# Upper levels of a triangular inverse on 64x64 blocks instead of 128x128 in a hybrid decoder on one core

## The chip, the core and the metric

The kernel runs on one core of a Trainium2 chip, written in the Tile framework: the engines' instruction streams are laid out at build time by a scheduler, which follows the program's data dependences, a few orders pinned by hand, and its own estimate of what is ready first. At run time each engine works through its list in that order and waits where an operand or a buffer is not there. The engines are TensorE (PE, with its weight loads shown as PEld), VectorE (DVE), ScalarE (ACT) and GpSimd (POOL); SyncE (SP) issues the DMAs. The metric is device time in microseconds (us); the median over several runs counts.

## What is computed

The reference is a decoder trunk of two layers on x of 256 positions x 1024 channels. Each layer adds half a SwiGLU feed-forward, then a mix of four head groups, then another half feed-forward:

```
x = x + 0.5 * rms_norm(swiglu(h, w_gate, w_up, w_down), post_g)      # twice a layer, around:
p = h @ w_in
y_a = gate_b * causal_depthwise_conv(gate_c * xa, sc_conv_w)         # group A
y_b = spatial_gating(u, v, ...)                                       # group B
y_c = rwkv7_time_mix(pc, ...)                                         # group C: 4 heads of 64
zd  = causal_depthwise_conv(z1 * sigmoid(z2), cm_conv_w) + cm_conv_b  # group D: 31 taps
y_d = silu(layer_norm(zd, ...))
m   = concatenate([y_a, y_b, y_c, y_d]) @ w_out
```

Group C holds the recurrence in which the change lies:

```
sa = einsum("bhij,bhj->bhi", state, a_t)
state = state * w_t + sa[..., None] * b_t + v_t[..., None] * k_t
y = einsum("bhij,bhj->bhi", state, r_t)
```

## The kernel before

The 256 positions are two blocks (b = 0, 1) of 128. Every large product is made of three f32r matmuls with weights and activations split in a high and a low part (mm3, L148 to L150); ACT makes the high part of a weight (whi, L140) and DVE the low part (wlo, L141), from DMA buffers named raw. These casts go on all the time, for the stage that comes next too.

In the mix the recurrence of a block is solved in parallel form. c_pair builds, per head, 128x128 matrices: pp (L607) on row tiles of 64, masked into PB and PK. The inverse of a unit triangular 128x128 matrix is needed for each of 4 heads x 2 blocks. c_base solves its 16x16 diagonal blocks on DVE and writes them, transposed, into XM (L652). c_level(4), (5) and (6) then double the block size, 16 to 32, 64 and 128. A level is, for each block: zp = PB times XM (c_z, L670, four matmuls of 128x128, one a head), a copy zz on ACT (L673), wps = XT times zz (c_w, L685), and a write of the new off-diagonal blocks into XM, at level 4 by DVE under a mask (L692), at level 5 by two small ACT copies (L695). tx transposes the new XM on PE (xtp, L663) and ACT copies it to XT (L664). At level 6 only the transposed result is wanted, wps of L682, and ACT writes it straight to XT (L689).

Behind the levels comes a serial chain: c_u (x, L715, and u, L724), c_state (sp, S), the same of the second block, c_y (yp, L755 to L758), the group norm of yp (statistics st L767 and mv on DVE, rgn on POOL, yn on DVE, L773), its transposes ynT in c_out (L782), oc, and the product yh, yl that the output projection wo reads (emit_y, L437, L438). Group D shares the engines: its 31-tap convolution is a list of DVE steps (zc, L829), then zcT transposes (L835), a layer norm (dlnmv on DVE, dln on POOL, tk L838) and znT transposes (L842). Group B's gating needs sg matmuls (L898) and tk on DVE (L904).

wo has 96 matmuls of 512 columns a layer: per block, eight slices of 128 channels, in the order A, B, D, C (the list KORD at the foot of the file), two halves, three matmuls each. They are ready as soon as their group's yh and yl are, and the scheduler puts them where the chain leaves PE free. Program order around the change is: c_base, c_level(4), b_in(0), a_out(0), c_level(5), a_out(1), c_level(6), c_u, c_state, c_u, b_in(1), c_y twice, d_conv, c_out(1), d_out(0), c_out(0), d_out(1), wout.

Of the kernel before, what the change touches and what calls it, by code (L numbers as in the profile page):

```python
# [48 lines left out]
def trunk_kernel(ctx: ExitStack, tc: tile.TileContext, a, out):  # L49
# [48 lines left out]
    masks = const.tile([P, 3, P], U8, name="masks")  # L98
# [6 lines left out]
    def late_constants():  # L105
        mraw = work.tile([P, 3, P], mybir.dt.int32, name="mraw", tag="c2", bufs=C2)
        later(mraw, a["masks"])
        nc.vector.tensor_copy(masks, mraw)
# [300 lines left out]
    def mix(l, nxt):  # L409
# [18 lines left out]
        XM = zero_tile([P, NB, 4, P], "XM")  # L428
        XT = wp.tile([P, NB, 4, P], F32, name="XT", tag="w2", bufs=10)
# [191 lines left out]
        def c_base():  # L621
# [36 lines left out]

        def tx(b):
            S = R[b]  # L660
            tp = acc_bank("xtp")
            for h in range(4):
                nc.tensor.transpose(tp[:, h * P:(h + 1) * P], S["Xm"][:, h, :], ident)  # L663
            nc.scalar.copy(S["XT"], tp.rearrange("p (h t) -> p h t", h=4))  # L664

        def c_z(b):
            S = R[b]
            zp = acc_bank("zp")
            for h in range(4):
                nc.tensor.matmul(zp[:, h * P:(h + 1) * P], lhsT=PB[b][:, h, 1, :], rhs=S["Xm"][:, h, :],  # L670
                                 start=True, stop=True)
            z = work.tile([P, 4, P], F32, name="zz", tag="c2", bufs=C2)
            nc.scalar.copy(z, zp.rearrange("p (h t) -> p h t", h=4))  # L673
            S["z"] = z

        def c_w(b, i):
            S = R[b]
            w = acc_bank("wps")
            last = i == 6
            for h in range(4):  # L680
                if last:
                    nc.tensor.matmul(w[:, h * P:(h + 1) * P], lhsT=S["z"][:, h, :], rhs=S["XT"][:, h, :],  # L682
                                     start=True, stop=True)
                else:
                    nc.tensor.matmul(w[:, h * P:(h + 1) * P], lhsT=S["XT"][:, h, :], rhs=S["z"][:, h, :],  # L685
                                     start=True, stop=True)
            wv = w.rearrange("p (h t) -> p h t", h=4)
            if last:
                nc.scalar.copy(S["XT"][0:64, :, 64:P], wv[0:64, :, 64:P])  # L689
                return  # L690
            if i == 4:
# [431 lines left out]
```

## Time and profile before

| | |
|---|---|
| median of three runs | 1040.91 us (1040.3 to 1043.53) |
| profiled execution | 1042.24 us, span 1040.5 us, granted clock 0.998 |
| PE busy | 1016.9 us, 98% of the span |
| DVE, ACT, POOL busy | 670.5, 536.8, 68.8 us |
| levels of layer 1 | 280.03 us (first transpose) to 298.52 us (first x) |
| yn of the second block, layer 1 | starts at 315.87 us |
| last wo, first pgu of the next feed-forward | 332.07 and 332.30 us |

The span is the profiled stretch on the core, the execution's own time 1.74 us more. Layer 2 shows the same stretch 512 us later. The granted clock is that of TensorE as a share of full speed.

### The profile page before, as it was taken

The numbers are of one execution on the slowest core, as the hardware profiler recorded it, in microseconds if no ns is written. First come the engines' busy times: TensorE is split into PE (matmuls) and PEld (weight loads), VectorE is DVE, ScalarE is ACT, GpSimd is POOL, SyncE is SP. The second block draws the span as 40 slices with busy tenths as digits, with TensorE's granted clock in tenths as the row PEclk, the third lists the DMA queues.
The fourth block names the chain that finished last, engine by engine and source line by source line (L and its number), as shares of the span: only waits on it lengthen the run. The fifth ranks groups of instructions, "written<-read, shape, count | busy, mean of one in ns | idle before, by whom it ended". The sixth has DMA issues, their size and how long they took to land.

```text
span 1040.5 us, 13557 instructions
## 1 busy us (share of the span) xinstructions
PE 1016.9 (98%) x4898; PEld 831.4 (80%) x4898; DVE 670.5 (64%) x1084; ACT 536.8 (52%) x864; POOL 68.8 (7%) x133
## 2 busy tenths in 40 slices
PE   8999999999999999999999999999999999999997
PEld 6878888888797788888887888887878877888885
DVE  6664645689988746464675464547999885645442
ACT  7554444567466545444555454436655664535331
POOL 1000000210012100000010000003000130000000
PEclk9999999999999999999999999999999999999999
DMA  7984646344045756564647564635522366556521
GB/s 277 295 274 161 214 150 223 91 168 152 20 154 174 223 191 194 169 206 159 202 145 220 181 203 161 212 133 160 171 89 82 115 196 235 178 186 186 179 81 40
DMA packets 51474, 178.28 MB, mean 171 GB/s; under 512 B 6096, under 2 KB 6608, under 8 KB 51408
## 3 DMA queue, kind: packets, MB, share of 16 engines
q1 hardware_dynamic: 51120, 176.91, 52.1%
q8 instruction: 38, 0.62, 0.2%
q10 hardware_dynamic: 288, 0.52, 0.1%
q14 instruction: 28, 0.23, 0.1%
HBM read 176.36 MB, written 1.05 MB: 170 GB/s over the span
## 4 chain that ended last, share of the span: by engine, by line
PE 82%; DVE 7%; DMA 4%; ACT 2%; issue 2%; POOL 1%; SPq 1%; DVEq 0%; POOLq 0%; ACTq 0%
PE pgu L148 13%; PE pgu L149 13%; PE pgu L150 13%; PE dn L148 8%; PE dn L149 7%; PE dn L150 7%; DMA raw<-in_ffn 4%; PE pin L149 3%; PE pin L148 3%; PE pin L150 3%; PE hTp L344 2%; DVE wlo L141 1%; PE zp L670 1%; PE wo L148 1%; PE xT L178 1%
## 5 line engine op out<-in xcount | busy, mean ns | idle before, releaser
L141 DVE TENSOR_TENSOR wlo<-raw,whi 128x1024 fp32r<-128x1024 f32 (+1 forms) x320 | 389.0, 1219 | 135.5 <-ACT whi L140 121.2
L140 ACT CAST whi<-raw 128x1024 fp32r<-128x1024 f32 (+1 forms) x320 | 334.3, 1047 | 169.3 <-DMA raw<-in_ffn 76.7
L148 PE MATMUL pgu<-whi,xh 128*128 128x512 f32 x704 | 279.7, 398 | 1.8 <-ACT xh L237 1.5
L149 PE MATMUL pgu<-wlo,xh 128*128 128x512 f32 x704 | 276.5, 393 | 1.0 <-DVE wlo L141 0.8
L150 PE MATMUL pgu<-whi,xl 128*128 128x512 f32 x704 | 275.6, 392 | 0.0
L148 PEld LDWEIGHTS pgu<-whi,xh 128*128 128x128 f32 x704 | 132.6, 188 | 30.0 <-ACT xh L237 1.8
L150 PEld LDWEIGHTS pgu<-whi,xl 128*128 128x128 f32 x704 | 132.7, 188 | 28.7
L149 PEld LDWEIGHTS pgu<-wlo,xh 128*128 128x128 f32 x704 | 132.7, 188 | 28.3 <-DVE wlo L141 1.1
L148 PE MATMUL dn<-whi,hh 128*128 128x512 f32 x352 | 142.8, 407 | 2.7 <-ACT hh L347 2.7
L149 PE MATMUL dn<-wlo,hh 128*128 128x512 f32 x352 | 139.8, 397 | 0.0
L150 PE MATMUL dn<-whi,hl 128*128 128x512 f32 x352 | 138.2, 394 | 0.0
L335 ACT ACTIVATE silu<-pgu,rpre 128x256 f32<-128x256 f32 x88 | 41.6, 472 | 137.7 <-PE pgu L150 136.5
L337 DVE SCALAR_TENSOR_TENSOR h<-pgu,rpre,silu 128x256 f32<-128x256 f32 x88 | 42.4, 481 | 101.8 <-ACT silu L335 101.7
L348 DVE TENSOR_TENSOR hl<-hTp,hh 128x256 fp32r<-128x256 f32 x88 | 36.9, 419 | 89.4 <-ACT hh L347 89.4
L347 ACT CAST hh<-hTp 128x256 fp32r<-128x256 f32 x88 | 32.5, 369 | 97.4 <-PE hTp L344 97.4
L148 PEld LDWEIGHTS dn<-whi,hh 128*128 128x128 f32 x352 | 66.2, 188 | 18.2 <-ACT hh L347 4.0
L150 PEld LDWEIGHTS dn<-whi,hl 128*128 128x128 f32 x352 | 65.9, 188 | 17.2 <-DVE hl L348 1.5
L149 PEld LDWEIGHTS dn<-wlo,hh 128*128 128x128 f32 x352 | 66.2, 188 | 13.8 <-DVE wlo L141 0.4
L149 PE MATMUL pin<-wlo,xh 128*128 128x512 f32 (+2 forms) x192 | 70.8, 371 | 0.0
L148 PE MATMUL pin<-whi,xh 128*128 128x512 f32 (+2 forms) x192 | 70.5, 371 | 0.0
L150 PE MATMUL pin<-whi,xl 128*128 128x512 f32 (+2 forms) x192 | 70.5, 371 | 0.0
L829 DVE SCALAR_TENSOR_TENSOR zc<-zT,par,zc 128x256 f32<-128x256 f32 x120 | 49.9, 478 | 3.2 <-ACT zc L826 3.1
(216 smaller groups left out, 914.6 us busy)
## 6 DMA issues: line engine op xcount, KB each, us to landing
raw<-in_ffn SPq DMA_DIRECT2D x260, 512.0 KB, 4.6
raw<-in_wout SPq DMA_DIRECT2D x16, 512.0 KB, 4.3
raw<-in_win_z SPq DMA_DIRECT2D x8, 512.0 KB, 4.4
raw<-in_win_rk SPq DMA_DIRECT2D x8, 512.0 KB, 4.4
raw<-in_win_ca SPq DMA_DIRECT2D x8, 512.0 KB, 3.7
raw<-in_win_uv SPq DMA_DIRECT2D x8, 512.0 KB, 4.5
gp<-in_post_g SPq DMA_DIRECT2D x6, 512.0 KB, 4.7
raw<-in_win_vl SPq DMA_DIRECT2D x8, 384.0 KB, 3.1
```

The costliest lines, as they stand in the source:

```text
L140: i0 = nc.scalar.copy(hi[:, 0:n], raw[:, 0:n])
L141: i1 = nc.vector.tensor_tensor(out=lo[:, 0:n], in0=raw[:, 0:n], in1=hi.bitcast(F32)[:, 0:n], op=ALU.subtract)
L148: nc.tensor.matmul(dst, lhsT=sh, rhs=hi[:, c0:c0 + n], start=start, stop=False)
L149: nc.tensor.matmul(dst, lhsT=sh, rhs=lo[:, c0:c0 + n], start=False, stop=False)
L150: nc.tensor.matmul(dst, lhsT=sl, rhs=hi[:, c0:c0 + n], start=False, stop=stop)
L178: t = nc.tensor.transpose(tp[:, k * P:(k + 1) * P], x[b][:, kk * P:(kk + 1) * P], ident)
L335: nc.scalar.activation(out=s, in_=pg[:, 0:256], func=AF.Silu, scale=r)
L337: nc.vector.scalar_tensor_tensor(out=h, in0=pg[:, 256:512], scalar=r, in1=s, op0=ALU.mult, op1=ALU.mult)
L344: nc.tensor.transpose(tp[:, j * P:(j + 1) * P], h[:, j * P:(j + 1) * P], ident)
L347: nc.scalar.copy(hh, tp[:, 0:256])
L348: nc.vector.tensor_tensor(out=hl, in0=tp[:, 0:256], in1=hh.bitcast(F32), op=ALU.subtract)
L829: nc.vector.scalar_tensor_tensor(out=zc[:, j, :], in0=zT[:, j, k:k + 256], scalar=w, in1=zc[:, j, :], op0=ALU.mult, op1=ALU.add)
```

## The change

XM becomes a compact tile of 64 columns per head: the two 64x64 diagonal blocks of a head stand above one another, rows 0 to 63 and 64 to 127. XT stays a full tile and is now zeroed, since only its blocks are written. In levels 4 and 5 the matmuls work on 64x64 pieces: each of the array's four 64x64 quarters has its own piece, by the rows that its operands stand on and by the rows of the PSUM bank that it writes, so a head's two pieces and the heads go round all four, and write two banks instead of one (zp0, zp1; wps0, wps1). tx takes the compact XM of two heads as one 128x128 transpose, two a block instead of four, into a small tile xt2. tx_last, ahead of level 6, makes the transposes by 64x64 matmuls with the identity, so that they land in XT's diagonal blocks. Level 6 has one 64x64 product per head for z and one for w, all on the same quarter of the array. Level 4's mask, called near, covers 64 columns, and level 4 writes with two smaller predicated copies per block, level 5 with four ACT copies per block where there were two.

```diff
-        XM = zero_tile([P, NB, 4, P], "XM")
-        XT = wp.tile([P, NB, 4, P], F32, name="XT", tag="w2", bufs=10)
+        XM = work.tile([P, NB, 4, 64], F32, name="XM", tag="XM", bufs=1)
+        nc.gpsimd.memset(XM, 0.0)
+        XT = zero_tile([P, NB, 4, P], "XT")
...
         def tx(b):
             S = R[b]
             tp = acc_bank("xtp")
+            for g in range(2):
+                nc.tensor.transpose(tp[:, g * P:(g + 1) * P],
+                                    S["Xm"][:, 2 * g:2 * g + 2, :].rearrange("p h c -> p (h c)"), ident)
+            t = c256("xt2")
+            nc.scalar.copy(t, tp[:, 0:256])
+            S["X2"] = t.rearrange("p (g e c) -> p g e c", g=2, e=2)
+
+        def tx_last(b):
+            S = R[b]
+            tp = acc_bank("xtp")
             for h in range(4):
-                nc.tensor.transpose(tp[:, h * P:(h + 1) * P], S["Xm"][:, h, :], ident)
-            nc.scalar.copy(S["XT"], tp.rearrange("p (h t) -> p h t", h=4))
-
-        def c_z(b):
+                for e in range(2):
+                    nc.tensor.matmul(tp[half(e), 64 * h:64 * h + 64], lhsT=S["Xm"][half(e), h, :],
+                                     rhs=ident[half(e), half(e)], start=True, stop=True)
+            for e in range(2):
+                nc.scalar.copy(S["XT"][half(e), :, half(e)], tp[half(e), 0:256].rearrange("p (h c) -> p h c", h=4))
+
+        def c_z(b, i):
             S = R[b]
-            zp = acc_bank("zp")
+            if i == 6:
+                zp = acc_bank("zp")
+                for h in range(4):
+                    nc.tensor.matmul(zp[64:P, 64 * h:64 * h + 64], lhsT=PB[b][0:64, h, 1, 64:P],
+                                     rhs=S["Xm"][0:64, h, :], start=True, stop=True)
...
+            zp = [acc_bank("zp0"), acc_bank("zp1")]
             for h in range(4):
-                nc.tensor.matmul(zp[:, h * P:(h + 1) * P], lhsT=PB[b][:, h, 1, :], rhs=S["Xm"][:, h, :],
-                                 start=True, stop=True)
-            z = work.tile([P, 4, P], F32, name="zz", tag="c2", bufs=C2)
-            nc.scalar.copy(z, zp.rearrange("p (h t) -> p h t", h=4))
+                for e in range(2):
+                    c0 = 64 * (h // 2)
+                    nc.tensor.matmul(zp[e][half(h % 2), c0:c0 + 64], lhsT=PB[b][half(e), h, 1, half(e)],
+                                     rhs=S["Xm"][half(e), h, :], start=True, stop=True)
+            z = work.tile([P, 2, 2, 64], F32, name="zz", tag="c1", bufs=C1)
+            for e in range(2):
+                nc.scalar.copy(z[:, e], zp[e][:, 0:P].rearrange("p (g c) -> p g c", g=2))
             S["z"] = z
...
+            w = [acc_bank("wps0"), acc_bank("wps1")]
             for h in range(4):
...
+                for e in range(2):
+                    hh = half(h % 2)
+                    c0 = 64 * (h // 2)
+                    nc.tensor.matmul(w[h % 2][half(e), c0:c0 + 64], lhsT=S["X2"][hh, h // 2, e, :],
+                                     rhs=S["z"][hh, e, h // 2, :], start=True, stop=True)
+            for m in range(2):
+                wv = w[m][:, 0:P].rearrange("p (g t) -> p g t", g=2)
+                xv = S["Xm"].rearrange("p (g m) t -> p m g t", m=2)[:, m]
+                if i == 4:
+                    nc.vector.copy_predicated(out=xv, mask=near.unsqueeze(1).broadcast_to([P, 2, 64]), data=wv)
                 else:
-                    nc.tensor.matmul(w[:, h * P:(h + 1) * P], lhsT=S["XT"][:, h, :], rhs=S["z"][:, h, :],
-                                     start=True, stop=True)
...
+                    for q in (32, 96):
+                        nc.scalar.copy(xv[q:q + 32, :, 0:32], wv[q:q + 32, :, 0:32])
+            (tx if i == 4 else tx_last)(b)
```

The new shapes and durations give the scheduler another order. Three places of it matter below. On DVE, at level 4 (XM is the inverse being built, ao and yl belong to group A), the list was:

```order
L876 SCALAR_TENSOR_TENSOR ao<-caT,par,ao 128x128
L141 TENSOR_TENSOR wlo<-raw,whi 128x1024
L692 COPY_PREDICATED XM<-masks,wps 128x512
L879 TENSOR_TENSOR ao<-ao,gbT 128x256
L141 TENSOR_TENSOR wlo<-raw,whi 128x1024 x2
L692 COPY_PREDICATED XM<-masks,wps 128x512
```

and is now:

```order
L729 COPY_PREDICATED XM<-near,wps_2511 128x2x64
L729 COPY_PREDICATED XM<-near,wps_2512 128x2x64
L913 SCALAR_TENSOR_TENSOR ao<-caT,par,ao 128x128
L143 TENSOR_TENSOR wlo<-raw,whi 128x1024
L729 COPY_PREDICATED XM<-near,wps_2528 128x2x64
L729 COPY_PREDICATED XM<-near,wps_2529 128x2x64
L916 TENSOR_TENSOR ao<-ao,gbT 128x256
L143 TENSOR_TENSOR wlo<-raw,whi 128x1024 x2
```

The copies of the second block moved ahead of a product of group A and of two weight casts.

On DVE, from the convolution zc to the statistics st of yp (tk of L904 and L941 is group B's gating), the list was:

```order
L829 SCALAR_TENSOR_TENSOR zc<-zT,par,zc 128x256 x19
L141 TENSOR_TENSOR wlo<-raw,whi 128x1024
L904 SCALAR_TENSOR_TENSOR tk<-sg,par,uvt 128x64 x4
L141 TENSOR_TENSOR wlo<-raw,whi 128x1024
L800 BN_STATS st_2934<-zcT 128x6
L801 BN_AGGR dlnmv<-st_2934 128x2
L438 TENSOR_TENSOR yl_1750<-ybT,yh_1748 128x256
L838 TENSOR_SCALAR tk<-zcT,dlnmv,dln 128x256
L141 TENSOR_TENSOR wlo<-raw,whi 128x1024
L800 BN_STATS st_2988<-zcT 128x6
```

and is now, up to the second block's yn and a little beyond:

```order
L866 SCALAR_TENSOR_TENSOR zc<-zT,par,zc 128x256 x8
L941 SCALAR_TENSOR_TENSOR tk<-sg,par,uvt 128x64 x4
L866 SCALAR_TENSOR_TENSOR zc<-zT,par,zc 128x256 x3
L441 TENSOR_TENSOR yl_1753<-ybT,yh_1751 128x256
L866 SCALAR_TENSOR_TENSOR zc<-zT,par,zc 128x256 x8
L143 TENSOR_TENSOR wlo<-raw,whi 128x1024 x3
L804 BN_STATS st<-yp 128x6 x4
L806 BN_AGGR mv<-st 128x2 x4
L143 TENSOR_TENSOR wlo<-raw,whi 128x1024
L810 TENSOR_SCALAR yn<-yp,mv,rgn 128x64 x4
L804 BN_STATS st<-yp 128x6 x4
L806 BN_AGGR mv<-st 128x2 x4
```

The convolution ends later against the rest, and the layer norms of zcT, which stood ahead of yp's statistics, stand behind the first yn.

On PE, around the transposes of yn (12 wo matmuls of the first block, yh_1747, stand between the last yp and znT, of which the last three are shown), the list was:

```order
L149 MATMUL wo<-wlo,yh_1747 128x512
L150 MATMUL wo<-whi,yl_1749 128x512
L148 MATMUL wo<-whi,yh_1747 128x512
L842 MATMUL znT<-ident,tk 128x128 x2
L149 MATMUL wo<-wlo,yh_1747 128x512
L150 MATMUL wo<-whi,yl_1749 128x512
L782 MATMUL ynT<-ident,yn 128x128 x3
L148 MATMUL wo<-whi,yh_1748 128x512
L782 MATMUL ynT<-ident,yn 128x128
```

and is now:

```order
L795 MATMUL yp<-us,PB_1740 128x128
L872 MATMUL zcT<-ident,zc 128x128
L819 MATMUL ynT<-ident,yn 128x128 x4
L150 MATMUL wo<-whi,yh_1751 128x512
L151 MATMUL wo<-wlo,yh_1751 128x512
L152 MATMUL wo<-whi,yl_1753 128x512
L879 MATMUL znT<-ident,tk 128x128 x2
L872 MATMUL zcT<-ident,zc 128x128 x2
L150 MATMUL wo<-whi,yh_1751 128x512
```

The wo matmuls between yp and ynT are gone from there (12 ahead of znT and two behind it); 72 of the 96 stand behind ynT now, 60 did. All four znT and the second block's zcT follow ynT.

## Rows read from the trace of the kernel before

**Rows 1.** The page: PE's busy time, and the chain that ended last.

```profile
PE 1016.9 (98%) x4898; PEld 831.4 (80%) x4898; DVE 670.5 (64%) x1084; ACT 536.8 (52%) x864; POOL 68.8 (7%) x133
...
PE 82%; DVE 7%; DMA 4%; ACT 2%; issue 2%; POOL 1%; SPq 1%; DVEq 0%; POOLq 0%; ACTq 0%
```

**Rows 2.** Windows: us, busy us and instructions by engine, clock, DMA, GB/s.

```profile
280.00:331.00 51.00, 49.48 (x329) 42.80 (x330) 45.35 (x105) 34.69 (x64) 8.40 (x16) 1.00 0.44 136
280.00:298.50 18.50, 18.47 (x142) 16.94 (x143) 18.44 (x43) 13.39 (x24) 1.11 (x3) 1.00 0.35 115
```

**Rows 3.** Timeline of PE, levels: start us, us, what, count, idle before.

```profile
280.03 1.09 PE L663 MATMUL xtp<-ident,XM 128*128 128x128 f32 x8 [1.24 <-DVE XM L652]
280.96 1.95 PE L670 MATMUL zp<-XM,PB 128*128 128x128 f32 x16
...
294.35 0.66 PE L663 MATMUL xtp<-ident,XM 128*128 128x128 f32 x4
...
298.52 1.06 PE L715 MATMUL x<-vt,PK 128*128 128x128 f32 x8
```

**Rows 4.** Timeline of DVE from the gating to yn of the second block.

```profile
300.51 0.85 DVE L904 SCALAR_TENSOR_TENSOR tk<-sg,par,uvt 128x64 f32<-128x64 f32 x4
...
309.28 0.62 DVE L767 BATCH_NORM_STATS2 st<-yp 128x6 f32<-128x64 f32 x4
...
315.87 1.10 DVE L773 TENSOR_SCALAR yn<-yp,mv,rgn 128x64 f32<-128x64 f32 x4 [0.98 <-POOL rgn L155]
```

**Rows 5.** Timeline of PE from yp to the end of wo.

```profile
311.68 0.47 PE L149 MATMUL wo<-wlo,yh 128*128 128x512 f32 x1
...
314.94 0.44 PE L842 MATMUL znT<-ident,tk 128*128 128x128 f32 x2 [0.26 <-DVE tk L838]
...
316.62 0.52 PE L782 MATMUL ynT<-ident,yn 128*128 128x128 f32 x3 [0.77 <-DVE yn L773]
...
332.07 0.39 PE L150 MATMUL wo<-whi,yl 128*128 128x512 f32 x1
```

**Rows 6.** Timeline of PE and PEld around the row tiles (pp).

```profile
259.45 0.58 PE L539 MATMUL gx<-hind,sq 128*128 128x4 f32 x4
...
261.70 1.13 PE L607 MATMUL pp<-pc 64*128 64x256 f32 x8
...
261.69 0.73 PEld L607 LDWEIGHTS pp<-pc 64*128 64x128 f32 x8 [0.17 <-issue]
...
267.94 0.19 PEld L898 LDWEIGHTS sg<-tk,sgw 128*128 128x128 f32 x1 [0.33 <-issue]
```

**Rows 7.** Timeline of DVE in the levels.

```profile
283.95 0.74 DVE L692 COPY_PREDICATED XM<-masks,wps 128x512 f32<-128x512 uint8 x1
...
284.91 2.36 DVE L141 TENSOR_TENSOR wlo<-raw,whi 128x1024 fp32r<-128x1024 f32 x2
287.18 0.73 DVE L692 COPY_PREDICATED XM<-masks,wps 128x512 f32<-128x512 uint8 x1
...
291.85 7.60 DVE L829 SCALAR_TENSOR_TENSOR zc<-zT,par,zc 128x256 f32<-128x256 f32 x19
```

**Rows 8.** Groups of ACT copies: count | busy us, mean ns | idle before.

```profile
L673 ACT COPY zz<-zp 128x512 f32<-128x512 f32 x12 | 7.0, 586 | 2.4 <-PE zp L670 2.4
...
L695 ACT COPY XM<-wps 32x128 f32<-32x128 f32 x8 | 2.1, 258 | 1.2 <-PE wps L685 1.1
```

**Rows 9.** Timeline of POOL: first steps of the norm of yp (rgn).

```profile
310.27 1.14 POOL L154 TENSOR_SCALAR rgn<-mv 128x4 f32<-128x4 f32 x1 [0.37 <-DVE mv L769]
...
314.55 0.19 POOL L154 TENSOR_SCALAR rgn<-mv 128x4 f32<-128x4 f32 x1 [2.03 <-DVE mv L769]
```

**Rows 10.** Windows of the first feed-forward, where PE idles.

```profile
4.00:8.00 4.00, 2.15 (x7) 0.91 (x5) 2.33 (x6) 2.86 (x7) 0.00 (x0) 1.00 0.86 267
8.00:12.00 4.00, 3.89 (x10) 3.10 (x11) 3.29 (x9) 3.26 (x10) 0.00 (x0) 0.57 1.06 403
64.00:67.00 3.00, 1.11 (x6) 0.66 (x5) 1.95 (x3) 1.45 (x4) 0.00 (x0) 1.00 0.96 329
```

More of the change, by code (lines that the diff above doesn't have):

```diff
@@ L97, in trunk_kernel @@
     keep_warm(7)
-    masks = const.tile([P, 3, P], U8, name="masks")
+    masks = const.tile([P, 2, P], U8, name="masks")
+    near = const.tile([P, 64], U8, name="near")
     eye = const.tile([P, 8, 16], F32, name="eye")
@@ L107, in late_constants @@
         later(mraw, a["masks"])
-        nc.vector.tensor_copy(masks, mraw)
+        nc.vector.tensor_copy(masks, mraw[:, 0:2])
+        nc.vector.tensor_copy(near, mraw[:, 2, 0:64])
         later(eye, a["eye"])
@@ L657, in c_base, with half @@
             return end
+        def half(e):
+            return slice(64 * e, 64 * e + 64)
         def tx(b):
@@ new lines, in c_z @@
+        def c_z(b, i):
+            S = R[b]
+            if i == 6:
[3 more added lines that the diff above has]
+                                     rhs=S["Xm"][0:64, h, :], start=True, stop=True)
+                z = c256("zz")
+                nc.scalar.copy(z[64:P, :], zp[64:P, 0:256])
+                S["z"] = z
+                return
+            zp = [acc_bank("zp0"), acc_bank("zp1")]
+            for h in range(4):
+                for e in range(2):
[5 more added lines that the diff above has]
+                nc.scalar.copy(z[:, e], zp[e][:, 0:P].rearrange("p (g c) -> p g c", g=2))
@@ L677, in c_w @@
             S = R[b]
-            w = acc_bank("wps")
-            last = i == 6
-            for h in range(4):
-                if last:
-                    nc.tensor.matmul(w[:, h * P:(h + 1) * P], lhsT=S["z"][:, h, :], rhs=S["XT"][:, h, :],
-                                     start=True, stop=True)
-                else:
-                    nc.tensor.matmul(w[:, h * P:(h + 1) * P], lhsT=S["XT"][:, h, :], rhs=S["z"][:, h, :],
[L686 to L691, printed above, removed]
-                nc.vector.copy_predicated(out=S["Xm"], mask=masks[:, 2:3, :].broadcast_to([P, 4, P]), data=wv)
-            else:
-                for q in (32, 96):
-                    nc.scalar.copy(S["Xm"][q:q + 32, :, q - 32:q], wv[q:q + 32, :, q - 32:q])
-            tx(b)
+            if i == 6:
+                w = acc_bank("wps")
+                for h in range(4):
+                    nc.tensor.matmul(w[0:64, 64 * h:64 * h + 64], lhsT=S["z"][64:P, 64 * h:64 * h + 64],
+                                     rhs=S["XT"][64:P, h, 64:P], start=True, stop=True)
+                nc.scalar.copy(S["XT"][0:64, :, 64:P], w[0:64, 0:256].rearrange("p (h t) -> p h t", h=4))
+                return
+            w = [acc_bank("wps0"), acc_bank("wps1")]
+            for h in range(4):
+                for e in range(2):
[8 more added lines that the diff above has]
+                    nc.vector.copy_predicated(out=xv, mask=near.unsqueeze(1).broadcast_to([P, 2, 64]), data=wv)
+                else:
+                    for q in (32, 96):
+                        nc.scalar.copy(xv[q:q + 32, :, 0:32], wv[q:q + 32, :, 0:32])
+            (tx if i == 4 else tx_last)(b)
         def own(bank):
@@ L703, in c_level @@
             for b in range(NB):
[L704 removed]
+                c_z(b, i)
             for b in range(NB):
```

5 lines of the change are left out of this document (2 added, 3 removed).

## The prediction

> **What bounds the kernel now.** I read the page first. TensorE (PE) is busy 98% of the span and the chain that ended last runs 82% over it [rows 1]: whatever PE does not have to do could be time. But a share of the whole span says nothing of the stage that the change touches, so I cut that stage out by windows. From the first transpose of the inverse to the end of the mix's projection, 280 to 331 us in layer 1, PE works 49.48 of 51 us; from 280 to 298.5, the levels themselves, VectorE (DVE) works 18.44 of 18.5 us too [rows 2]. So the stage has two full engines. They stay together because PE has filler: where a level waits for a copy, PE takes matmuls of the output projection (wo), 96 a layer, which must be done by 332.3 anyway. The saving is real only if PE still has something ready when the serial chain makes it wait.
>
> That chain is: levels, x, u, the state, yp, the normalised yn of the second block, its transposes ynT, and then what is left of wo. PE runs from the first transpose at 280.03 to the first x at 298.52, 18.5 us [rows 3]. yn of the second block starts at 315.87, behind a POOL step [rows 4], and ynT at 316.62 with 0.77 us of PE idle, the largest wait of the tail; the last wo starts at 332.07 [rows 5]. Layer 2 repeats this 512 us later, so every term counts twice.
>
> **PE's own work.** An f32 matmul leaves two records. The 16 records of zp (8 matmuls of 128 columns) take 1.95 us [rows 3]; 0.16 or so of that is the last one's end beyond its turn, so they start 0.112 apart. Per layer the levels hold 24 transposes and 48 matmuls, that is 24 + 96 records, and a transpose takes the same 0.112 (8 in 1.09 us with the end): 120 x 0.112 = 13.4 us. After it there are 8 transposes (0.9) and 96 matmuls of 64x64, 192 records, of which 128 go to four tiles in turn in levels 4 and 5, 32 to two tiles (the last transposes), 32 to one tile (level 6).
>
> The trace holds no 64x64 matmul; bounds come from the nearest rows. Dearest: four records of only 4 columns also take 0.58 us, some 0.11 apart with the end [rows 6], so fewer columns alone need save nothing where 128 columns of weights are loaded; 192 x 0.112 = 21.5. Cheapest: the pp matmuls use 64 rows of the array, so two row tiles; 8 records of 256 columns take 1.13 us [rows 6], with the same end taken off 0.12 each, about what zp's records take with half the columns. So two tiles do run at the same time. With half the columns a 64x64 record should cost half of 0.112, 0.056, when alone on its tile, and a quarter of that with four tiles at work. I take: levels 4 and 5, 128 x 0.056 / 4 = 1.8; last transposes 32 x 0.056 / 2 = 0.9; level 6, 32 x 0.056 = 1.8; sum 4.5. Without concurrency it would be 192 x 0.056 = 10.8. I stay near the cheap end because pp is the nearest row (same tiling in one direction).
>
> Going between whole array and tiles costs. Into pp the weight loads idle 0.17 us, out of it 0.33 [rows 6]; part of that any load waits behind a matmul, so 0.50 for there and back is the upper end and nothing the lower. I take 0.35. The changed order goes there and back 7 times a layer: 2.4 us (0 to 3.5). PE work after: 0.9 + 4.5 + 2.4 = 7.8 us, 5.6 saved. Bounds: 8.0 saved with free switches; 0.7 lost without concurrency (0.9 + 10.8 + 2.4 = 14.1); 11.4 lost if each record kept 0.112.
> The Trainium skill, "TensorEngine Tiling (Array Packing)", Key Properties, says that changing the tiling mode drains TensorE; those idle loads agree. Its section Instruction Overhead gives each matmul about 60 cycles, which 64 columns just exceed; by that page the records are not dearer than I take them, and the sum is unchanged.
>
> **The chain through the levels.** Level 4: now the second predicated copy starts at 287.18, behind one product and two wlo of 2.36 us together [rows 7], and ends at 287.91. The changed DVE order puts all four small copies ahead of those two wlo. A 128x512 copy takes 0.73; two of 128x128, with a fixed part as in ACT's copies (0.26 for 32x128 against 0.59 for 128x512 [rows 8]), some 0.33 each. The level ends at about 285.0, 2.9 us earlier. Level 5: ACT makes eight small copies of 0.21 to 0.26 [rows 8] where there were four, and two casts of 1.05 stand between; I lay it out as 6.8 us where it was 6.4 (287.91 to 294.35, the last transposes [rows 3]): +0.4. Level 6: 3.75 for 4.2 (294.35 to 298.52), -0.45. x then starts 3.0 us earlier, at 295.5. That is far less than the 5.6 PE saves, because this chain is copies and semaphores.
>
> **From there to yn.** Now 315.87 - 298.52 = 17.35 us. DVE sets it, and its list ahead of yn is another one: the convolution's 19 steps in a row (7.60 us, 0.40 each [rows 7]) used to come before the four tk of the gating; now 8 come ahead of them and 3 and 8 behind, followed by three wlo in a row and only then the statistics of yp. From x's start: 1.4 to tk, which needs the gate product sg behind x's 0.89 us on PE; tk 0.85 [rows 4], three steps 1.2, yl 0.4, eight steps 3.2, three wlo at 1.22 3.65, and from the statistics to yn 6.6 as now (309.28 to 315.87 [rows 4]): 17.3, the same. So yn starts at 312.8. A check without PE: ahead of yn DVE has one wlo (1.13), one tk of the convolution (0.5), one statistics (0.4), one yl (0.4) and 0.1 of predicated copy less, 2.6 us, plus a wait of 0.4 to 1.5; so 2.6 to 4.1 earlier. I take 3.0.
>
> **From yn to the end of wo.** Now 332.3 - 315.87 = 16.4 us. By the changed PE order 72 wo stand behind ynT where 60 did: the 12 that run from 311.68 until znT at 314.94 [rows 5]. Those needed nothing of the chain but were the output of the convolution; the changed DVE order finishes the convolution's last eight steps and its transposes so late that both zcT of the second block and all four znT now come after ynT, and the wo on them with it. So PE, which saves work, loses its filler: yp ends at about 308.3 and ynT starts at 312.8 + 0.75 = 313.55; PE stands idle for about 5 us. Behind ynT: 12 x 0.23 = 2.7 (the last one started at 332.07 and the next matmul at 332.30); six transposes 0.7; znT of the first block waits for DVE (a wlo of 1.2 and tk 0.5) and POOL (the first of its two steps takes 0.19 alone but took 1.14 beside a wlo [rows 9]): it is ready 3.6 us after yn starts, PE gets there after 2.1, 1.4 idle; znT of the second is ready 8.2 after, PE is there at 6.9, 1.3 idle. Together 6.1 us.
>
> **Sum.** Per layer -3.0 + 6.1 = +3.1, twice +6.2. The profiled execution took 1042.24 us (span 1040.5 and 1.74 around it), so 1048.4 in its terms; it stands 1.33 above the median 1040.91 of the three runs, and from the median I forecast 1047. The PE account agrees: 5.6 saved and 3.1 lost need 8.7 us more idle; 5.1 ahead of ynT and 2.7 at znT, less 1.0 that ends there now, give 6.8, and the rest falls between level 4 and 6.
> The new homes of XM and XT and the memset more on POOL I cost at nothing: they lie far ahead of the levels, under PE's projections; uncovered they would hold the levels up by one memset. The masks are made once, under the first FFN.
>
> **Rivals.**
> Faster: the levels are bound by PE after all and shorten by the 5.6 it saves, not by 3.0. Then yp ends at 305.7, yn of the second block starts as far behind it as now (311.7 to 315.87, 4.2), at 309.9 or 6.0 earlier, and if PE, late enough, finds znT ready, only 3.4 come back: -2.6 a layer, 1036. 98% of PE [rows 1] speaks for it, DVE's 18.44 of 18.5 [rows 2] against it. It decides from yn before 312.4 without waits at znT, before 309.8 with them. More, up to 1030 (2 x 5.6), needs filler ahead of ynT, which the PE order does not hold. Chance 0.13, 1030 to 1037.8.
> No change: yn comes 4.1 earlier (the far end of the DVE check) and one of the znT waits vanishes: 6.1 - 1.4 - 4.1 = +0.6 a layer, 1042; 1037.8 to 1044. Chance 0.25.
> Dearer: tiles do not overlap. PE work is 14 instead of 7.8; half of the 6.2 lies under ACT's copies, the rest, 3.1, moves yn: 1047 + 6.2 = 1053. Or the pause lets the clock fall: after 4 to 8 us, where PE was busy 2.15 of 4 us, the granted clock averaged 0.57 over the next 4 us, most of them at the 1.2 GHz level [rows 10], which costs 0.43 x 4 = 1.7 us of work each time, +3.4, 1050; but at 64 to 67 with 1.89 idle it stayed 1.00. Chance of either 0.15, 1050 to 1057.
> By the Trainium skill, "TensorE: Matmul & The Clock Gate", Part 1, an idle TensorE is set back to half its clock; the fall at 8 us agrees, no row here has a pause of 5 us in a busy stage.
> That the change does nothing is out: the matmul shapes differ in the order.
>
> **How the numbers follow.** A measurement of this kernel tells about 0.3%, 3.1 us, from no change. Likeliest, +6.2 with its terms (switches 0 to 3.5, yn 2.6 to 4.1, waits at znT 1.3 to 2.7): 1044 to 1050, chance 0.47. With the cases above: faster 0.13, same 0.25, slower 0.62. The range leaves out most of the faster case and the dearest end: 1037 to 1054.
>
> **What would show it.** Right: 64x64 zp records starting under 0.03 us apart and some 6 us less PE busy per layer; x at about 295.5; yn of the second block near 312.8; a PE idle of 4 to 6 us ahead of ynT, waiting for yn; idle of 1 to 1.5 us ahead of each znT; pgu of the next stage near 335.4. Wrong: records 0.05 or more apart (tiles not concurrent), yn below 310 (DVE freed more than I count), wo found in the gap ahead of ynT, or a granted clock below 1.00 behind the pause.

## The result and the profile after

The changed kernel took 1050.05 us (median of 5 runs, 1049.12 to 1053.17) where the kernel before, on the same chip, took 1042.08: a ratio of 1.0075 (95% interval 1.0053 to 1.0097). It is slower, by 8.0 us. The profiled execution took 1049.12 us, its span is 1047.4 us.

First the page of the changed kernel: PE's busy time fell by 2.7 us against [rows 1] while the span grew by 6.9. PE is still 97% busy.

```profile
PE 1014.2 (97%) x5058; PEld 823.6 (79%) x5058; DVE 669.4 (64%) x1089; ACT 534.6 (51%) x884; POOL 70.6 (7%) x135
```

To find the place, the span is cut at the first transpose of the levels and at the first pgu of the next feed-forward, in both layers. Before, the pieces are 280.03, 52.27, 459.88, 52.22 and 196.10 us; after, 280.29, 56.23, 459.13, 56.24 and 195.51. So the whole loss is 3.96 and 4.02 us in the two stages that hold the change. Within the stage, counted from its first transpose (layer 1):

| us from the first transpose | before | after | moved |
|---|---|---|---|
| x starts (levels done) | 18.49 | 15.70 | -2.79 |
| convolution zc done | 19.42 | 22.89 | +3.47 |
| last yp ends (0.25 behind its last pair's start) | 31.76 | 28.91 | -2.85 |
| yn of the second block | 35.84 | 33.28 | -2.56 |
| ynT | 36.59 | 34.02 | -2.57 |
| first pgu of the next stage | 52.27 | 56.23 | +3.96 |

The levels gave 2.8 us, 2.6 of it reached yn, and behind yn 6.5 were lost (16.43 before, 22.95 after). The timeline of PE after, levels and tail (columns as in [rows 3]), shows both halves:

```profile
280.29 0.65 PE L671 MATMUL xtp<-ident,XM 128*128 128x128 f32 x4 [1.26 <-DVE XM L655]
280.88 1.04 PE L702 MATMUL zp<-XM,PB 64*64 64x64 f32 x32
281.71 0.62 PE L723 MATMUL wps<-zz,xt 64*64 64x64 f32 x16
...
291.88 1.07 PE L682 MATMUL xtp<-ident,XM 64*64 64x64 f32 x11 [0.15 <-ACT XM L732]
292.74 0.27 PE L692 MATMUL zp<-XM,PB 64*64 64x64 f32 x1
...
292.96 0.92 PE L692 MATMUL zp<-XM,PB 64*64 64x64 f32 x13
...
295.99 1.16 PE L752 MATMUL x<-vt,PK 128*128 128x128 f32 x8
...
306.27 0.39 PE L795 MATMUL yp<-us,PB 128*128 128x128 f32 x2
...
309.17 0.27 PE L872 MATMUL zcT<-ident,zc 128*128 128x128 f32 x1
314.31 1.10 PE L819 MATMUL ynT<-ident,yn 128*128 128x128 f32 x4 [4.87 <-DVE yn L810]
...
315.64 0.63 PE L151 MATMUL wo<-wlo,yh 128*128 128x512 f32 x1
316.06 0.63 PE L152 MATMUL wo<-whi,yl 128*128 128x512 f32 x1
317.19 0.69 PE L879 MATMUL znT<-ident,tk 128*128 128x128 f32 x2 [0.50 <-DVE tk L875]
...
336.52 0.39 PE L150 MATMUL pgu<-whi,xh 128*128 128x512 f32 x1
```

The 32 zp records take 0.83 us to the start of the wps behind them (281.71), 0.026 each; ahead of ynT PE idles 4.87 us, against 0.77 in [rows 5]. Behind it one wo takes 0.42 us to the next start (315.64 to 316.06) where it took 0.23, until about 320.2. The windows (columns as in [rows 2]) name the reason, in the third number from the end of a row:

```profile
280.20:331.20 51.00, 44.13 (x390) 35.67 (x390) 40.63 (x103) 31.83 (x70) 9.23 (x17) 0.93 0.37 125
...
312.00:314.00 2.00, 0.00 (x0) 0.00 (x0) 0.90 (x6) 0.58 (x1) 1.21 (x2) 0.87 0.06 25
314.00:316.00 2.00, 1.69 (x6) 1.44 (x7) 1.86 (x5) 1.17 (x4) 1.07 (x1) 0.50 0.00 0
...
318.00:320.00 2.00, 2.00 (x7) 1.62 (x6) 2.00 (x7) 1.33 (x4) 0.11 (x1) 0.50 0.49 150
320.00:322.00 2.00, 2.00 (x10) 1.62 (x9) 1.26 (x5) 1.67 (x3) 0.84 (x2) 0.93 0.59 229
```

TensorE had been idle since 309.4; the granted clock fell to 0.50, the 1.2 GHz level, before ynT started. Of the stage's 51 us PE works 44.1 where it worked 49.5 [rows 2], in spite of the slower tail. DVE after, at the places of [rows 4] and [rows 7]:

```profile
284.61 0.49 DVE L729 COPY_PREDICATED XM<-near,wps 128x128 f32<-128x128 uint8 x2
...
297.41 0.86 DVE L941 SCALAR_TENSOR_TENSOR tk<-sg,par,uvt 128x64 f32<-128x64 f32 x4 [2.34 <-PE sg L935]
...
307.04 0.62 DVE L804 BATCH_NORM_STATS2 st<-yp 128x6 f32<-128x64 f32 x4
...
313.57 1.10 DVE L810 TENSOR_SCALAR yn<-yp,mv,rgn 128x64 f32<-128x64 f32 x4 [1.10 <-POOL rgn L157]
...
316.59 0.54 DVE L875 TENSOR_SCALAR tk<-zcT,dlnmv,dln 128x256 f32<-128x256 f32 x1 [0.73 <-POOL dln L157]
```

The last copy of level 4 is done 4.8 us into the stage instead of 7.9. At 297.41 DVE, with eleven convolution steps and three casts still ahead, waits 2.34 us for the gate product sg; that is new. The first block's yp is there at 306.52 (its last pair starts at 306.27, plus 0.25), and its statistics start at 307.04, right behind three casts, with no wait of their own. tk of group D, which znT needs, stands behind the second yn. Last, PE's groups that make up the levels (both layers; count, busy us, mean ns of one, idle), of the kernel before:

```profile
L670 PE MATMUL zp<-XM,PB 128*128 128x128 f32 x96 | 11.7, 275 | 0.0
L685 PE MATMUL wps<-zz,XT 128*128 128x128 f32 x64 | 8.7, 279 | 0.0
L663 PE MATMUL xtp<-ident,XM 128*128 128x128 f32 x48 | 7.3, 282 | 2.5 <-DVE XM L652 2.5
L682 PE MATMUL wps<-XT,zz 128*128 128x128 f32 x32 | 4.1, 281 | 0.0
```

and after:

```profile
L723 PE MATMUL wps<-zz,xt 64*64 64x64 f32 x128 | 5.4, 231 | 0.0
L682 PE MATMUL xtp<-ident,XM 64*64 64x64 f32 x64 | 5.0, 233 | 0.3 <-ACT XM L732 0.3
L702 PE MATMUL zp<-XM,PB 64*64 64x64 f32 x128 | 4.4, 229 | 0.0
L671 PE MATMUL xtp<-ident,XM 128*128 128x128 f32 x16 | 2.9, 283 | 3.0 <-DVE XM L655 2.5 <-DVE XM L729 0.5
L692 PE MATMUL zp<-XM,PB 64*64 64x64 f32 x32 | 2.3, 221 | 0.0
L714 PE MATMUL wps<-XT,zz 64*64 64x64 f32 x32 | 2.3, 221 | 0.0
```

31.8 us became 22.3: 4.75 a layer.

### The profile page after: what moved, and what is told of

The parts are those of the page before. It is cut to its first block, busy times and chain, and to the rows that moved or that the text cites. A ratio compares the mean times of both kernels' runs of the same rounds, so it can differ in the third digit from the quotient of the medians.

```text
span 1047.4 us, 13904 instructions
## 1 busy us (share of the span) xinstructions
PE 1014.2 (97%) x5058; PEld 823.6 (79%) x5058; DVE 669.4 (64%) x1089; ACT 534.6 (51%) x884; POOL 70.6 (7%) x135
## 3 DMA queue, kind: packets, MB, share of 16 engines
HBM read 176.36 MB, written 1.05 MB: 169 GB/s over the span
## 4 chain that ended last, share of the span: by engine, by line
PE 82%; DVE 8%; ACT 3%; DMA 3%; issue 2%; POOL 1%; SPq 0%; DVEq 0%; POOLq 0%; ACTq 0%
PE pgu L151 14%; PE pgu L150 14%; PE pgu L152 14%; PE dn L150 8%; PE dn L151 8%; PE dn L152 8%; DMA raw<-in_ffn 3%; PE pin L151 3%; PE pin L152 3%; PE pin L150 3%; PE hTp L346 2%; ACT whi L142 2%; DVE wlo L143 1%; PE wo L151 1%; PE wo L152 1%
```

## The experiments

My theory (A in the expectations) was the prediction's: the new order leaves PE without wo ahead of ynT, and the tail pays for it. Against it stood that the 64x64 matmuls themselves cost the time (B), that the fallen clock makes most of the loss (C), and, after the first runs, that whatever of group D stands ahead of the chain is paid back in a later yn (D), or that pins alone are worth the gain (E). In the expectations, "the same" means pinned for pinned_tp and before_pinned, and ynt_tp for d0_early_tp.

Each kernel was timed beside the kernel before. All measured values in one table; the stage runs from the first transpose of the levels to the first pgu, yn is the second block's, from the stage's start, and the idle is PE's ahead of ynT (layer 1).

| kernel | median, ratio (95%) | stage, layers 1, 2 | x | yn | idle at ynT |
|---|---|---|---|---|---|
| before | 1042.08 | 52.27, 52.22 | 18.49 | 35.84 | 0.77 |
| after | 1050.05, 1.0075 (1.0053 to 1.0097) | 56.23, 56.24 | 15.70 | 33.28 | 4.87 |
| d_early | 1050.34, 1.0073 (1.0052 to 1.0093) | 56.29, 54.86 | 15.70 | 38.63 | 2.4 |
| before_late_d | 1055.97, 1.0131 (1.0116 to 1.0146) | 58.97, 58.70 | 18.47 | 35.52 | 4.49 |
| warm_fill | 1051.61, 1.0083 (1.0067 to 1.0100) | 56.79, 56.34 | 15.70 | 33.90 | 1.11 |
| gate_late | 1053.18, 1.0102 (1.0085 to 1.0118) | 56.82, 56.22 | 15.69 | 33.60 | 5.09 |
| ynt_tp | 1057.20, 1.0126 (1.0094 to 1.0159) | 58.37, 58.31 | 15.69 | 34.16 | 1.18 |
| d0_early_tp | 1050.82, 1.0071 (1.0044 to 1.0098) | 52.94, 54.03 | 15.7 | 35.33 | 0.25 |
| before_d0_early_tp | 1050.94, 1.0070 (1.0048 to 1.0092) | 54.91, 54.85 | 18.5 | 36.80 | 1.38 |
| warm_wide | 1055.62, 1.0116 (1.0078 to 1.0154) | 58.90, 58.40 | 15.69 | 34.15 | 1.51 |
| pinned | 1048.14, 1.0066 (1.0040 to 1.0092) | 56.02, 55.78 | 15.69 | 37.32 | 3.66 |
| pinned_tp | 1049.95, 1.0085 (1.0067 to 1.0103) | 54.61, 54.71 | 15.7 | 37.31 | 1.17 |
| before_pinned | 1053.19, 1.0114 (1.0099 to 1.0129) | 57.68, 58.58 | 18.5 | 39.92 | 3.92 |
| d0_pinned | 1040.12, 0.9970 (0.9952 to 0.9987) | 51.00, 51.75 | 15.70 | 34.02 | 2.35 |

The causes are read from the stages: the stretch ahead of the first levels, which no run was meant to change, took 278.5 to 283.9 us in these profiles, and no run gives the reason.

**The kernel before with the late order of group D (before_late_d).** The 128x128 levels stay; only D moves, its zcT behind yp and its znT behind ynT.

```diff
-            for j in range(2):
-                nc.tensor.transpose(tp[...], zc[...], ident)
+            with tc.issue_after(R[1]["ye"].ins):       # the last yp
+                for j in range(2):
+                    nc.tensor.transpose(tp[...], zc[...], ident)
...
+            with tc.issue_after(R[0]["yt"].ins):       # znT behind the last ynT
...
             c_out(1)
+            c_out(0)
             d_conv(27, 31)
             d_out(0)
...
-            c_out(0)
             d_out(1)
```

> The kernel before, its levels on 128x128, but with group D's transposes put behind yp and ynT as the changed kernel has them (zcT after the last yp, znT after ynT), so that no wo of group D is left to fill the gap. Theory A: the same loss appears without any 64x64 matmul: a PE pause of about 4.5 us ahead of ynT, 12 more wo behind it, and 4 to 6 us a layer, so 1050 to 1054 us. Rival B: within 2 us of before, 1042, since the levels are unchanged.

It took 1055.97 us, a ratio of 1.0131: more than theory A's 1050 to 1054, with the pause that it expected. No wo stands between yp and ynT and 72 stand behind, as in the changed kernel. Its PE timeline and one window show the tail again:

```profile
317.56 0.87 PE L782 MATMUL ynT<-ident,yn 128*128 128x128 f32 x3 [4.49 <-DVE yn L773]
```

```profile
318.00:320.00 2.00, 2.00 (x8) 1.60 (x7) 1.27 (x3) 0.40 (x2) 1.63 (x2) 0.50 0.00 0
```

From yn to pgu it takes 23.45 us, the changed kernel 22.95, the kernel before 16.43. So the tail's loss needs no 64x64 matmul: group D's late order makes it. And at a like order the small blocks are worth 58.97 - 56.23 = 2.74 us in layer 1 and 2.46 in layer 2, about all that x is earlier.

**Group D all ahead (d_early, pinned).** Two ways to give the changed kernel its filler back: D written ahead of the last c_y, and then the same held there by pins (zcT of block 0 ahead of the state part of x, the rest ahead of the second block's u and yp, two weight casts behind D).

```diff
-            b_in(1)
+            gate = b_in(1)
+            d_conv(20, 31)
+            gate()
+            d_out(0)
+            d_out(1)
             c_y(0, None)
             c_y(1, S0)
-            d_conv(20, 27)
             c_out(1)
-            d_conv(27, 31)
-            d_out(0)
...
-            d_out(1)
```

> The changed kernel with another program order: the convolution's last steps and group D's layer norm are traced ahead of yp, and the gating of group B behind the convolution, so that the convolution runs through on DVE, and 12 wo of the first block stand ahead of ynT on PE again, as they did before the change. Theory A (the loss comes from filler that fell behind ynT, the 64x64 levels themselves are faster): the pause ahead of ynT shrinks from 4.9 to under 1.5 us, the granted clock stays at 1.00, yn of the second block starts near 312.5, the last wo ends near 329 in layer 1, and the time is about 1036 us, faster than before and 14 below the changed kernel. Rival B (the 64x64 matmuls, their weight loads and the switches between tiles and whole array cost what they save): no faster than before, 1042 us or more. Rival C (the fall of the clock is the loss): between, about 1040.

> The changed kernel with group D put back ahead of yp by hand: program order and pins keep the convolution, both layer norms and all zcT and znT ahead of or inside yp on PE, the norms' DVE steps ahead of yp's statistics, and the two weight casts that were waited for behind them. 14 wo stand between yp and ynT, all else as in the changed kernel. Theory A (64x64 shortens the levels by 2.8 us a layer, and the loss lies in group D coming after yn): x at 15.7 us after the first transpose, yn of the second block at 34, no wait at znT, no fall of the clock, 49 to 50 us from the first transpose to the end of wo where the kernel before takes 52.2: 1035 to 1038 us. Rival D (DVE and ACT are too full between the levels and yp for group D; whatever is put ahead delays yn): yn at 35 or later and stalls inside yp, 52 us or more: 1041 or more.

Theory A missed in both. In d_early rival B's time came (1042 or more), but not by its cause: x stands at 15.70 as in the changed kernel, yn came 5.3 us later, and PE waits in three places:

```profile
PE ynT L819 <- DVE yn L810: 2.4, 1, 2.4
PE znT L879 <- DVE tk L875: 2.2, 1, 2.2
...
PE wo L150 <- ACT yh L440: 0.9, 2, 0.7
```

pinned shows by what, in its DVE timeline: two weight casts and both yl of D stand between tk of D and the statistics of yp, which start 3.2 us later than in the changed kernel (29.91 behind the first transpose, there 26.75). Another 0.9 comes behind them: the first POOL step of the second block's norm takes 1.07 us beside a cast, 0.19 in the changed kernel. yn is at 37.32 instead of 33.28.

```profile
306.18 0.54 DVE L886 TENSOR_SCALAR tk<-zcT,dlnmv,dln 128x256 f32<-128x256 f32 x1 [0.95 <-POOL dln L157]
306.64 2.35 DVE L143 TENSOR_TENSOR wlo<-raw,whi 128x1024 fp32r<-128x1024 f32 x2
308.91 0.76 DVE L448 TENSOR_TENSOR yl<-yd,yh 128x256 fp32r<-128x256 f32 x2
309.58 0.62 DVE L815 BATCH_NORM_STATS2 st<-yp 128x6 f32<-128x64 f32 x4
```

Rival D holds for these two: all of D ahead of the chain is paid back in yn.

**Pairs at other orders (pinned_tp, before_pinned, d0_early_tp, before_d0_early_tp).** pinned_tp is pinned with ynT's PSUM bank from another pool, and before_pinned is pinned on the levels of before; d0_early_tp writes only D's first block ahead of c_y, with that same bank, and its pair puts that on the levels of before.

```diff
-            tp = acc_bank("ynT")
+            tp = tp_bank("ynT")
```

> The same with ynT in the pool of the small transposes, so that 23 wo stand between yp and ynT. Theory A: PE has no pause there at all; 47 to 48 us a layer: 1031 to 1035 us. Rival D: as the run above, 1041 or more.

> The kernel before, levels on 128x128, with the program order and pins of the first of these runs. Theory A: x at 18.5, yn at 36 to 37, 52 us a layer as before, 1041 to 1044: the pins by themselves bring nothing. Rival E: the pins are the gain, 1035 to 1038 here too.

> The same, and the convolution runs through ahead of group B's gating, with group D's first block traced ahead of yp: 23 wo stand between yp and ynT, the first znT ahead of them. Theory A: the pause is under 1 us, no wait at the first znT; yn of the second block is 1 to 1.5 us later than in the changed kernel, because DVE does group D first; from the first transpose of the levels to the end of wo some 48 us where it was 52.3 before the change: 1033 to 1037 us, faster than both kernels. Rival B: 1045 or more.

> The kernel before, levels on 128x128, with the program order and the bank of the run above. Theory A: PE was nearly full in this stretch (1.5 us idle of 51), so better filler can give back at most that: 1039 to 1042, and the run above is lower by the 2.5 us a layer that the 64x64 levels save: the change is worth something only with filler. Rival B: as fast as the run above or faster.

Theory A's numbers all missed: x is 2.8 us earlier in each of the changed kernels, but another wait follows. In d0_early_tp PE waits 2.7 us in the middle of wo, for ACT's yh. In pinned_tp 1.7 us come up at the first pgu and the stretch to the second layer's levels grew to 462.75 from 459.88. The pairs give the worth of the small blocks three times: stages shorter by 2.74 and 2.46 (late D), 1.97 and 0.82 (first block early), 1.66 and 2.80 (pinned). Never longer, never more than 2.8 a layer. The whole times follow in two pairs (1.0075 against 1.0131, 1.0066 against 1.0114) and not in the third: with the first block early the two kernels take the same time (1.0071 and 1.0070), as rival B said. In their profiles the stretches around the stages are 5.7 us longer in the changed kernel, and why stays open. Rival E, that the pins are the gain, does not hold: before_pinned is slower than before.

**Only DVE freed (gate_late).** The changed kernel with tk of the gating behind the convolution, so that DVE doesn't stand 2.34 us for sg.

```diff
-            b_in(1)
+            gate = b_in(1)
...
             d_conv(27, 31)
+            gate()
```

> The changed kernel with the four gating steps of group B traced behind the convolution, so that DVE does not stand 2.3 us waiting for the sg product but goes on with the convolution; the 12 wo and group D's transposes stay behind ynT. Theory A: yn of the second block starts 2 us earlier, at about 311.5, the pause is 2.9 us, the filler is still missing: 2 us a layer less, about 1046. Rival C: with a pause under 3 us the clock holds, and the time falls by 5 us a layer, to 1040.

Both numbers missed, and rival C's condition, a pause under 3 us, was not met: it is 5.09. The wait at sg went and yn came no sooner (33.60 for 33.28). The DVE timeline shows a wait of 3.42 us for ACT's whi in its place:

```profile
303.08 1.22 DVE L143 TENSOR_TENSOR wlo<-raw,whi 128x1024 fp32r<-128x1024 f32 x1
307.72 1.23 DVE L143 TENSOR_TENSOR wlo<-raw,whi 128x1024 fp32r<-128x1024 f32 x1 [3.42 <-ACT whi L142]
...
310.33 0.62 DVE L804 BATCH_NORM_STATS2 st<-yp 128x6 f32<-128x64 f32 x4
```

The casts behind that wait end 0.32 us later than in the changed kernel, so the statistics start 0.32 later (27.07 behind the first transpose for 26.75), and yn follows by the same 0.32. Nor could DVE alone have given the 2 us: from x to the first block's yp PE takes 10.5 us in both kernels (10.6 before), and in the changed one the statistics start only 0.5 behind it.

**Other wo into the gap (ynt_tp).** The one-line edit above, alone in the changed kernel: the scheduler then puts 20 wo into the gap.

> The changed kernel with one word changed: ynT takes its PSUM bank from the pool of two that the small transposes use, not from the four of the recurrence. Those stay free for the second block's projection, and the PE order now has 20 wo of the second block (groups A and B, which need nothing of the chain) between yp and ynT. Theory A (the pause ahead of ynT for want of filler is the loss): the pause of 4.9 us is gone, the clock holds, 4.6 us a layer come back, less what the waits at znT take again once the filler is used up (their work on DVE still comes after yn): 1040 to 1044 us. Rival B (64x64 and its switches cost what they save): PE waits elsewhere in the same amount and it stays near 1050.

The idle at ynT fell to 1.18 us, and the stage grew by 2.1:

```profile
PE znT L879 <- DVE tk L875: 3.6, 1, 3.6
PE zcT L872 <- ACT yd L882: 1.8, 1, 1.8
```

The wait moved to znT. That is rival B's "PE waits elsewhere", without its matmuls being the cause; both times missed (1057.20). Filler is a sum that is spent once: these wo were missing two steps on, and the clock fell there (0.50 from 325 to 327 us).

**A busy PE in the gap (warm_fill, warm_wide).** 20 matmuls of 4 columns, or 19 of 128, between the last yp and ynT, into an unused part of a bank, to leave the idle and take the clock's fall away.

```diff
+            if b == 0:
+                with tc.issue_after(R[1]["ye"].ins), tc.issue_after(tr.ins):
+                    for _ in range(20):
+                        W["fill"] = nc.tensor.matmul(tp[:, 256:260], lhsT=ones, rhs=ones[:, 0:4], ...)
+                        tc.keep_in_program_order(W["fill"])
```

> The changed kernel with 20 matmuls of 4 columns (40 records of about 0.11 us, 4.5 us in all, written to an unused part of the zcT bank) in the pause ahead of ynT, and the order of wo and znT behind it pinned as it was; they add nothing to the output. Theory A: PE has work through the pause and the granted clock stays at 1.00, but yn is ready no sooner, and PE, faster behind it, waits 1.4 us ahead of the first znT and about 1 ahead of the second; the time falls by under 1 us a layer, to 1048.5 to 1050. Rival C: the clock's fall costs half of the 5.7 us that PE worked at half speed, 2.8 us a layer: 1044.5.

> The changed kernel with 19 matmuls of 128 columns in the pause ahead of ynT (4.3 us, written to an unused part of a bank, adding nothing to the output), where the run with 4 columns left the granted clock low. Theory A: the clock holds at 1.00, yn is no sooner, the waits at znT grow to 1.4 us and more, and 1 us a layer comes back at most: 1048 to 1050 us. Rival C: the clock's fall is 2.8 us a layer of real loss: 1044.5.

Neither separates the clock from the order. With the narrow fill PE shows busy up to 1.11 us ahead of ynT, and the clock fell all the same:

```profile
309.74 4.53 PE L876 MATMUL zcT<-ones 128*128 128x4 f32 x40
...
315.38 0.87 PE L819 MATMUL ynT<-ident,yn 128*128 128x128 f32 x3 [1.11 <-DVE yn L810]
```

```profile
316.00:318.00 2.00, 1.75 (x6) 0.94 (x4) 1.27 (x2) 0.58 (x2) 1.54 (x2) 0.50 0.10 14
```

With the wide fill it stayed at 1.00 through the gap and fell later, behind idles of 1.51 us at ynT and 2.18 at znT; but the order of DVE had moved too, yn was 0.9 us later (the cast beside POOL's step again, 1.07 us), and the stage longer. The clock being up, PE came to the first znT earlier and waited longer, 2.18 us for 0.50. Theory A's range (to 1050) and rival C's 1044.5 both missed, with 1051.61 and 1055.62.

**Only half of D ahead (d0_pinned).** Of group D the first block alone is held ahead (zcT before the state part of x, znT behind the second block's u), the second stays behind yp; the two weight casts go behind the first tk.

```diff
+            gate = b_in(1)
+            d_conv(20, 31)
+            gate()
+            rest = d_out(0)              # up to tk; rest() is znT and what follows
             c_u(1, S0)
-            b_in(1)
+            with behind("u1"):
+                rest()
             c_y(0, None)
             c_y(1, S0)
-            d_conv(20, 27)
             c_out(1)
-            d_conv(27, 31)
-            d_out(0)
-            prep_out(2)
-            prep_out(3, "w2")
+            with behind("tk0"):
+                prep_out(2)
+                prep_out(3, "w2")
             c_out(0)
-            d_out(1)
+            with behind("ye"):
+                rest = d_out(1)
+            rest()
```

> The changed kernel's mathematics, with only the first block of group D held ahead: zcT of block 0 ahead of the state part of x, znT of block 0 behind u of the second block, the statistics of yp behind tk of block 0, and D of block 1 behind yp; 12 wo then stand between yp and ynT and seven more ahead of the second znT. Theory A (the tail loses because PE has no wo left ahead of ynT, and half of D ahead is cheap): yn of the second block 33.5 to 34 us behind the first transpose of the levels, wait at ynT at most 1.5 us with the granted clock at 1.00, stage 49 to 50 us where it was 52.3, total about 1036. Theory D (whatever of D stands ahead of the chain is paid back in yn): yn 35 or later, stage 52 or more, total 1041 or more.

It is the one version that beats both kernels: 0.9970 of the kernel before (0.9952 to 0.9987), 1040.12 us. Its PE timeline in layer 1, and at the same place in layer 2:

```profile
312.58 0.39 PE L152 MATMUL wo<-whi,yl 128*128 128x512 f32 x1
315.32 0.52 PE L829 MATMUL ynT<-ident,yn 128*128 128x128 f32 x3 [2.35 <-DVE yn L820]
...
318.20 0.44 PE L892 MATMUL znT<-ident,tk 128*128 128x128 f32 x2 [0.16 <-DVE tk L885]
...
331.56 0.39 PE L150 MATMUL pgu<-whi,xh 128*128 128x512 f32 x1
...
826.26 0.52 PE L829 MATMUL ynT<-ident,yn 128*128 128x128 f32 x3 [2.37 <-DVE yn L820]
```

Twelve wo stand between yp and ynT again (309.81 to 312.58), yn is only 0.74 us later than in the changed kernel, and from yn to pgu it takes 16.98 us, 6.0 less. yn is where the filler's theory had it (33.5 to 34), but the stage lies between the two theories and the time nearer to the bound of theory D (1041) than to 1036: I expected a stage of 49 to 50 and an idle of at most 1.5. yp ends 2.6 us earlier than before while yn, behind DVE and POOL, is only 1.8 earlier, so the same 12 wo no longer reach it. This order was not put on the old levels, so how much of the 0.3% is the small blocks' and how much the order's is not shown.

## Why the prediction was right, and where not

**Right: what decides is whether PE still has something ready.** The prediction said that the saving is real only then, that 12 wo lose their place between yp and ynT, and that PE would idle 4 to 6 us there. It idles 4.87. before_late_d shows the loss with the old levels, d0_pinned takes it back with the new ones. That the change makes the kernel slower follows from it. But one of its own signs of being wrong came too, a granted clock below 1.00 behind the pause, and the time, 3 us above the 1047 that it forecast, lies where its likeliest case ends and its dearer one begins.

**The levels.** Predicted: x 3.0 us earlier; measured 2.8, and far less than PE saves, as said. PE's own term was mis-sized: 5.6 a layer predicted, 4.75 by the groups. The zp records do start under 0.03 apart (0.026), but I had taken 0.056 / 4 = 0.014 for levels 4 and 5, so the prediction's "the records are not dearer than I take them" does not hold; the last transposes, for which I took 0.056 / 2, took 0.078 (11 records from 291.88 to 292.74), more than the 0.058 of level 6 (13 records in 0.92 us, 0.22 of it the last one's end; 0.056 predicted), where z's four heads share one quarter and w's another. These transposes stand in the path of level 6, which took 4.11 us (291.88 to 295.99), not 3.75; that they alone make the difference is not shown. The Trainium skill, "TensorE: Matmul & The Clock Gate", Part 1, has a floor of about 25 ns from one matmul's start to the next, however small; the 0.026 agrees. By an estimate from that floor 128 records would have been put at 3.2 us instead of 1.8. The Trainium skill, "TensorEngine Tiling (Array Packing)", Gotcha 1, says that different row tiles cannot work on one PSUM bank together; the last transposes write both row tiles into one bank and zp into two, which agrees, but no run here sets this apart.

**x to yn: right, row by row, with PE close behind.** Predicted 17.3 us, measured 17.58 (33.28 - 15.70). The statistics of yp start 11.05 us behind x (10.7 predicted; 0.44 of it is a wait of a cast for ACT's whi that I had not counted), and from there to yn it takes 6.53 (6.6 predicted). "DVE sets it" holds, since the statistics start right behind its casts, but by 0.5 us only: then PE's chain to the first block's yp would set it. So the list of DVE was not where 2 us could be had (gate_late). When all of D stands ahead, DVE's list is what makes yn late (pinned, 37.32).

**yn to pgu: right sum, two terms exchanged.** Predicted +6.1, measured 6.5. The 12 wo (2.7) and the transposes (0.7) are there. The two waits at znT, 2.7 together, shrank to 0.5: PE came too late to wait. In their place the granted clock fell behind the pause, which stood as a rival by itself, priced at 1.7. At the 1.2 GHz level from 314.3 to 320.2, less the 0.5 of idle, half of 5.4 us would be lost, 2.7; by difference to d0_pinned, (22.95 - 16.98) less 2.74 for the wo, 0.45 for two pairs of transposes (0.22 a pair at full clock, 301.52 to 301.74 in d0_pinned) and 0.34 of wait, it is 2.4. So the likeliest case and the clock's rival came together: 2.7 + 0.7 + 0.5 + 2.4 to 2.7 is 6.3 to 6.6. That a slow PE waits less is mechanism; that the two terms cancel to 0.4 us is luck.

**The sum.** +3.1 a layer predicted, +3.96 and +4.02 measured: 0.2 from x, 0.2 on the way to yn, 0.4 in the tail. The rival that PE's saving counts in full, the one that yn comes 4.1 earlier, and the one that the quarters don't overlap are all excluded by x at -2.8, yn at -2.6 and 0.026 a record.

**Open.** The clock's part was not taken away alone: both fills changed the order as well. What stands for it is the account above and two kernels whose layers have the same order and nearly the same idles, but not the same clock. In d0_pinned (idles of 2.35 and 2.37 us) it stayed at 1.00 in the first layer and ynT to pgu took 16.24 us; in the second it fell for some 3.4 us and they took 17.09 (826.26 to 843.35): 0.85 more, where half of 3.4 would be 1.7. In warm_wide PE worked some 5.5 us at the low level in layer 1 and 3.4 in layer 2; ynT to pgu took 24.01 and 23.06, 0.95 apart, where half of the difference is 1.05. So the fall costs time, but half of the time at the low level can be too much, and the 2.4 to 2.7 above stay an account. How much of it would return as waits at znT is open too.

## What to carry to other kernels

Where a full engine fills the waits of a serial chain with work that isn't on it, a faster chain is worth something only as long as that filler still stands in the longest wait: count the filler instructions ahead of each wait in the new order, not only the instructions saved. A scheduler redraws that order when durations change, so time the new mathematics together with a pinned order: here the same levels gave +0.75% and -0.3%. Put the old mathematics on the best order as well, which is missing here. Filler moved from one wait to another is missing there, and pulling a whole side group ahead of the chain delays the chain; half of it was the best here.

## What the runs showed of the hardware

A 64x64 f32 record cost 0.026 us over four quarters of the array, 0.058 on one quarter and 0.078 in the last transposes (two quarters, one PSUM bank); a 128x128 one 0.112 [rows 3].

POOL's first step of the group norm took 0.19 us alone and 1.07 beside a cast on DVE (312.24 in the changed kernel, 314.78 in pinned).

The granted clock fell to 0.50 behind idles of 4.87, 4.49 and 5.09 us, but also behind 4.5 us of four-column matmuls and an idle of 1.11 (warm_fill), although the records show PE busy through them. These windows of d0_pinned stand behind idles of 2.35 us in layer 1 and 2.37 in layer 2:

```profile
316.00:318.00 2.00, 2.00 (x10) 1.29 (x8) 1.28 (x2) 1.55 (x5) 1.48 (x2) 1.00 0.19 29
...
827.00:829.00 2.00, 2.00 (x7) 1.51 (x6) 1.27 (x2) 1.25 (x4) 1.42 (x2) 0.50 0.12 18
```

So the length of an idle alone did not tell whether the clock would fall.
